# A depthwise convolution's second channel chunk moves to TensorE as products with diagonal matrices, beside attention in a two-layer backbone

## The chip, the cores and the metric

The kernel runs on one core of a Trainium2 chip. The metric is the device time of one execution in microseconds (us), lower is better. A core has TensorE (PE in the profile; PEld is its weight loads), VectorE (DVE), ScalarE (ACT), GpSimd (POOL) and SyncE (SP, which here issues most of the transfers). Each engine works through its own queue in order.

## The reference, cut to what matters

Two layers, shared by 512 latent and 128 context tokens, with 1024 channels:

```python
h = _rms(x, norm_g[0]) * (1 + sc1) + sh1
x = x + 0.5 * g1 * _swiglu(h, ffn1_wi, ffn1_wo)
h = _rms(x, norm_g[1]) * (1 + sc2) + sh2
u = h @ w_in                                   # 1536 columns
o_pool = _pool_mixer(u[..., :256], ...)
o_conv = _conv_mixer(u[..., 256:768], ...)
o_attn = attention(u[..., 768:])               # 8 heads, 5 blocks of 128 queries
x = x + g2 * (concat([o_pool, o_conv, o_attn]) @ w_out)
h = _rms(x, norm_g[2]) * (1 + sc3) + sh3
x = x + 0.5 * g3 * _swiglu(h, ffn2_wi, ffn2_wo)

def _conv_mixer(g, dw, db, norm_g, pw):
    glu = g[..., :256] * sigmoid(g[..., 256:])
    y = depthwise_conv(glu, dw, taps=31, centred) + db     # per channel
    return silu(_rms(y, norm_g)) @ pw
```

The nine vectors `sh1 ... g3` of a layer are SiLU(cond) @ mod_w + mod_b; each is 1024 columns of a 1024-row matrix.

## The kernel before, in words

Channels lie on the 128 partitions and tokens along the free dimension, so the 256 channels of the convolution are two chunks (c = 0 and 1). A dense product is done with a high and a low part of each operand in the type float32r, three products each (`product`, line 368). A layer is a feed-forward stage, the mixer (`mixer`, line 789), and a second feed-forward stage.

The mixer first makes the convolution's gate and value, keys, values and half of the queries from `u` (`ORDER`, line 54). Then it goes through 20 steps: four query chunks c, each with the five query blocks of `BATCHES` as two batches (line 1162 on). `batch` (line 1062) is attention's chain: scores on PE (L1085), mask and maximum on DVE (L1088), exponential on ACT (L1096), sum and reciprocal on DVE (L1097, L1098), scaling on ACT (L1100), transposes on PE (L1103) and their copies on ACT (L1104), products with the values on PE (L1110). It is written with a higher priority than what is laid beside it: the other half of the queries (q1), the pooling (pl), and the first part of the output product over w_out (`out_chunks`, part 0, tiles p_a and p_b), all paced by `PLAN`. The rest of w_out (tile p, L748) comes behind the 20 steps, with the second feed-forward stage.

Three more things ride on the steps, and the change touches all three:

- **Modulation.** Sixteen pieces of mod_w (vectors 5, 7, 6, 8; four pieces each), paced by `FILL` (line 44). A piece is a transfer of 1 MB issued on SP into one of two buffers (tag "raw", shared with the w_in and w_out loads) and eight float32 products (L269) into the one PSUM bank with the tag "x" (`BANKS`, line 46). After four pieces DVE reads the bank out.
- **Taps.** `conv_taps` (line 925) adds 31 shifted, scaled copies of the gated input `glu` into `cy`, one tile of 128x655 for each chunk; the 655 columns are 512 latent and 128 context tokens with 15 zero columns between. `TAP_PLAN` says how many taps of which chunk go with each step, and `behind` ties a tap to the batch's last reciprocal on DVE (chunk 0) or its last copy on ACT (chunk 1). Chunk 0 and the last four taps of chunk 1 are one DVE instruction each (L935; the first tap is L933). Taps 1 to 26 of chunk 1 are a scaled copy on ACT (L938, tile cm) and an add on POOL (L939):

```python
elif c == 0 or tp > POOL_TAPS:
    V.scalar_tensor_tensor(out=y, in0=src, scalar=wt, in1=y, ...)
else:
    A.activation(out=m, in_=src, func=AF.Copy, scale=wt)
    G.tensor_tensor(out=y, in0=y, in1=m, op=ALU.add)
```

- **The rest of the convolution.** `convolution` (line 1022) starts at step `CONV_AT` = 15 and does one piece per step: squares (L1024, L1025, tiles cacc and csq), the sum over channels on PE (L322, rc_ss), the spread of the scale (L334, rc_a and rc_b), swish, and the pointwise product (tiles cp_a, cp_b).

POOL also does rotary products for the queries (L824, L825) and the pooling sums (L980 to L988). A scheduler sets the order of each engine's queue from the written order and the priorities.

Of the kernel before, what the change touches and what calls it, by code (L numbers as in the profile page):

```python
# [9 lines left out]
F32 = mybir.dt.float32  # L10
F32R = mybir.dt.float32r
I32 = mybir.dt.int32
AF = mybir.ActivationFunctionType
ALU = mybir.AluOpType
PSUM = bass.MemoryType.PSUM

P = 128
# [10 lines left out]
TAPS = 31  # L28
# [8 lines left out]
COUT = NLAT + CPAD + NCTX  # L37
PPAD = 8
PLEN = PPAD + NLAT + PPAD + NCTX + PPAD
TMP = 688  # L40

FILL = (1, 0, 1, 1, 1, 1, 2, 1, 1, 2, 1, 1, 2, 1, 0, 1, 1, 2, 2, 1)
FILL_MODS = ((5, 7, 6, 8), (), (5, 7, 6, 8))
BANKS = {"a": 3, "s": 2, "t": 1, "o": 1, "x": 1}
AHEAD = 200
NOW = 400
BEHIND_BY = 0
BUFS = {"act": 6, "tmp": 7, "half": 9, "w": 3, "raw": 2}  # L50
POOL_TAPS = 26
CONV_AT = 15
TAP_PLAN = ((3, 2, 1, 2, 3, 2, 0, 2, 2, 1, 3, 2, 0, 2, 1, 3, 1, 1, 1, 3), (2, 4, 3, 3, 4, 4, 4, 2, 0, 4, 1, 1, 0, 1, 2, 1, 2, 0, 1, 4))
ORDER, BEHIND = ("cg", "kv", "q0", "ca"), ("q1", "pl")
PLAN = (0, 1, 0, 1, 0, 2, 0, 1, 0, 0, 0, 1, 1, 1, 2, 1, 1, 1, 1, 0)

# [42 lines left out]
def backbone(ctx: ExitStack, tc: tile.TileContext, ins, consts, y_prompt, y_sample, out_k, out_v):  # L99
    nc = tc.nc  # L100
    V, A, G, PE = nc.vector, nc.scalar, nc.gpsimd, nc.tensor
# [4 lines left out]
    scope = {}  # L106
# [12 lines left out]
    def bank(name, tag="o"):  # L119
        return psum.tile([P, 512], F32, tag=tag, name=name, bufs=BANKS[tag])  # L120
# [12 lines left out]
    def act(shape, dt, name):  # L133
        return work.tile(shape, dt, tag="act", name=name, padded_shape=[P, 2, T] if len(shape) == 3 else [P, 2 * T], bufs=BUFS["act"])
# [7 lines left out]
    ident = con[:, C_ID - C_EDGE:C_ID - C_EDGE + P]  # L142
# [4 lines left out]
    def transposed(rows, name, srcs, queue):  # L147

        t = tmp(name + "_r", P)
        for r0, src in srcs:  # L150
            n = src.shape[0]
            queue.dma_start(out=t[r0:r0 + n, 0:src.shape[1]], in_=src)
        ps = bank(name + "_ps")
        PE.transpose(ps[:, :rows], t[:rows, :], ident[:rows, :rows])
        o = one.tile([P, rows], F32, name=name)
        V.tensor_copy(o, ps[:, :rows])
        return o
# [15 lines left out]
    def bias_of(l, queue):  # L173
# [3 lines left out]
    vec = transposed(60, "vec", [  # L177
        (0, ins["norm_g"].rearrange("l j (k p) -> (l j k) p", p=P)),
        (48, ins["pool_scale"].rearrange("l (k p) -> (l k) p", p=P)),
        (52, ins["conv_b"].rearrange("l (k p) -> (l k) p", p=P)),  # L180
        (56, ins["conv_norm_g"].rearrange("l (k p) -> (l k) p", p=P)),
    ], nc.scalar)
# [17 lines left out]
    for i in range(5):  # L200
        xt = act([P, D], F32, f"xt{i}")
        src = ins["x_sample"][0, i * P:(i + 1) * P, :] if i < 4 else ins["x_prompt"][0]
# [83 lines left out]
    def mod_steps(l, vs, summed=True):  # L286
        return [f for v in vs for f in modulation(l, v, summed)]
# [478 lines left out]
    def into_ffn(l, j, wi, nm, load, mv, gate):  # L766

        acc = tmp(f"acc{l}{j}")
        inp = Input(l, j)
        scale_of(l, j, inp.a)  # L770
        f = Ffn(l, j, inp, wi)

        def then(h, sq):
            if h:
                plain_products(f, 0)
            with tc.high_priority(offset=NOW):
                pb = rstd_half(acc, sq, h, f"r{l}{j}{h}")
                for kp in range(4):
                    (inp.second if h else inp.first)(pb, kp)
            if h:  # L780
                for kp in range(4):
                    inp.sums(kp)
                plain_products(f, 1)

        last_group(nm, load, mv, gate, acc, then)
        return f


    def mixer(l, xa, R, tab, fill):
        w_in = ins["w_in"][l]  # L790
        taps, qkg, sink, nsink = (par[n] for n in ("taps", "qkg", "sink", "nsink"))
# [114 lines left out]
        glu = []  # L906
# [12 lines left out]

        QS, rq = {}, {}  # L920

        ys = [scope["pool"].tile([P, COUT], F32, tag="sg", name=f"cy{l}{c}", padded_shape=[P, TMP], bufs=3) for c in range(2)]
        todo = [list(range(TAPS)), list(range(TAPS))]

        def conv_taps(c, n, behind=None):

            for tp in todo[c][:n]:
                y = ys[c]
                wt = taps[:, (l * TAPS + tp) * 2 + c:(l * TAPS + tp) * 2 + c + 1]
                src = glu[c][:, tp:tp + COUT]  # L930
                with tc.issue_after(behind.ins) if behind is not None else ExitStack():
                    if tp == 0:
                        V.tensor_scalar(out=y, in0=src, scalar1=wt, scalar2=vec[:, 52 + 2 * l + c:53 + 2 * l + c], op0=ALU.mult, op1=ALU.add)  # L933
                    elif c == 0 or tp > POOL_TAPS:
                        V.scalar_tensor_tensor(out=y, in0=src, scalar=wt, in1=y, op0=ALU.mult, op1=ALU.add)  # L935
                    else:
                        m = scope["pool"].tile([P, COUT], F32, tag="sg", name=f"cm{l}{tp}", padded_shape=[P, TMP], bufs=3)
                        A.activation(out=m, in_=src, func=AF.Copy, scale=wt)  # L938
                        G.tensor_tensor(out=y, in0=y, in1=m, op=ALU.add)  # L939
            del todo[c][:n]  # L940

        def query_heads(t, b, c):
            sq, qt = tmp(f"qsq{l}{c}"), tmp(f"qt{l}{c}")
# [217 lines left out]
        i = 0  # L1161
        for c in range(4):
            m = act([P, 2, T], F32R, f"mixa{l}{c}")
            mix[4 + c] = (m[:, 0, :], m[:, 1, :])
            for blks in BATCHES:
                with tc.high_priority(offset=AHEAD):
                    behind = batch(c, blks, m)
                for _ in blks:
                    for _ in range(FILL[i]):
                        if fill:  # L1170
                            with tc.high_priority(offset=-BEHIND_BY):
                                fill.pop(0)()
                    for cc in range(2):
                        conv_taps(cc, TAP_PLAN[cc][i], behind[cc])
                    if i == CONV_AT:
                        for cc in range(2):
                            conv_taps(cc, TAPS, behind[cc])
                        conv = convolution()
                    if i >= CONV_AT:
                        next(conv, None)  # L1180
                    for _ in range(PLAN[i]):
                        next(bg)
                    i += 1
# [28 lines left out]
    f = Ffn(0, 0, inp, ins["ffn1_wi"][0])  # L1212
# [38 lines left out]
    for l in range(DEPTH):  # L1251
# [26 lines left out]
        ffn(f, ins["ffn1_wo"][l], gate1, after1, fill)  # L1278
        R = rstd(st["acc"], float(D), f"r{l}1")
        f = mixer(l, st["xa"], R, st["tab"], mod_steps(l, (5, 7, 6, 8), False))  # L1280

        g3 = gate_of(l, 2, 0.5)
# [15 lines left out]
        if not last:  # L1298
# [6 lines left out]
            f = into_ffn(l + 1, 0, ins["ffn1_wi"][l + 1], f"o{l}2_3", load, lambda k: (hid[lo + k][:, 0, :], hid[lo + k][:, 1, :]), g3)  # L1305
# [27 lines left out]
```

## Time and profile before

| | us |
|---|---|
| median of 3 runs | 2453.72 (2448.52 to 2455.20) |
| the profiled execution | 2454.21 |
| its span in the trace | 2452.4 |
| PE busy, share of the span | 2340.1, 95% |
| DVE busy | 1706.3, 70% |
| ACT busy | 1023.1, 42% |
| POOL busy | 462.5, 19% |

The span runs from the first to the last instruction; the execution's own time is 1.8 us longer. A busy PE is not PE at its densest: matmuls are pipelined, and a matmul counts as busy from its start to its modelled end. The mixer's steps lie around 570 to 755 us in layer 0 and 1775 to 1968 us in layer 1.

### The profile page before, as it was taken

To read this page: it belongs to the slowest core of one execution; us is meant where nothing else is said; L and a number is where in the kernel's file an instruction comes from. 1 tells how busy PE (TensorE), PEld (TensorE's weight loads), DVE (VectorE), ACT (ScalarE), POOL (GpSimd) and SP (SyncE) were. 2 spreads that over 40 slices of the span, in tenths; PEclk is the share of its full clock that TensorE was granted. 3 is DMA by queue.
4 is the path that set the end of the run, shared out by engine and by line. 5 is a ranking of instruction groups with operands and counts; after the bars stand their busy time and mean duration, and the time that the engine had idled before them with its cause. 6 is when DMAs were issued, how large, how long until landed. Compare 5 with 4: busy or idle time off the path is not lost.

```text
span 2452.4 us, 40409 instructions
## 1 busy us (share of the span) xinstructions
PE 2340.1 (95%) x16479; PEld 2218.7 (90%) x16479; DVE 1706.3 (70%) x3160; ACT 1023.1 (42%) x1867; POOL 462.5 (19%) x369
## 2 busy tenths in 40 slices
PE   7999999999789899999989999999997889999999
PEld 6999999997568899999989999999974789999998
DVE  7649495858866857585778585857588669585855
ACT  5324242426664533333354242424357545242423
POOL 2102020202531202020131111112024222020210
PEclk8999999999989999999999999999998899999999
DMA  7442422323402133333312424223243022222222
GB/s 236 140 154 83 142 83 75 100 91 123 163 22 78 52 115 123 112 117 118 115 41 85 142 82 142 78 86 102 73 149 129 31 70 81 75 82 91 78 78 78
DMA packets 193989, 246.03 MB, mean 100 GB/s; under 512 B 5705, under 2 KB 176494, under 8 KB 193804
## 3 DMA queue, kind: packets, MB, share of 16 engines
q1 hardware_dynamic: 191824, 240.81, 30.0%
q8 instruction: 129, 2.11, 0.4%
q0 software_dynamic: 512, 1.95, 0.3%
q10 hardware_dynamic: 1468, 0.70, 0.1%
q14 instruction: 56, 0.46, 0.1%
HBM read 240.55 MB, written 2.88 MB: 99 GB/s over the span
## 4 chain that ended last, share of the span: by engine, by line
PE 82%; DVE 11%; ACT 4%; issue 2%; DMA 1%; POOL 0%; SPq 0%; ACTq 0%; DVEq 0%
PE f_B L560 11%; PE o_a L378 11%; PE f_C L560 11%; PE f_A L560 11%; PE o_b L378 11%; PE f_D L560 6%; PE f L601 3%; PE p L748 2%; PE mod L269 2%; DVE cy L935 1%; PE u_q_b L378 1%; PE u_q_a L378 1%; DVE xa_l L396 1%; PE o L748 1%; ACT a_2S L1096 1%
## 5 line engine op out<-in xcount | busy, mean ns | idle before, releaser
L378 PE MATMUL o_a<-f_h,o_wh 128*128 128x320 f32 x1344 | 403.7, 311 | 0.0
L378 PE MATMUL o_b<-f_h,o_wh 128*128 128x320 f32 x1344 | 401.8, 310 | 0.0
L420 DVE SCALAR_TENSOR_TENSOR X<-o_a,gate,X 128x320 f32<-128x320 f32 x120 | 65.8, 549 | 303.6 <-PE o_a L378 303.3
L378 PEld LDWEIGHTS o_a<-f_h,o_wh 128*128 128x128 f32 x1344 | 251.2, 188 | 8.7 <-ACT o_wh L357 5.8
L357 ACT ACTIVATE o_wh<-wo 128x768 fp32r<-128x768 f32 (+1 forms) x120 | 95.9, 801 | 380.8 <-PE o_b L378 258.2
L378 PEld LDWEIGHTS o_b<-f_h,o_wh 128*128 128x128 f32 x1344 | 251.2, 188 | 2.9 <-issue 2.9
L552 POOL TENSOR_TENSOR f_t<-f 128x512 f32<-128x512 f32 x80 | 126.1, 1576 | 664.7 <-DMA f<-in_ffn_wi_dram 472.0
L659 POOL TENSOR_TENSOR f_t<-f_t,f 128x512 f32<-128x512 f32 x80 | 111.1, 1389 | 638.8 <-DVE f_q_wl L538 333.4
L378 PE MATMUL o_b<-f_h,o_wl 128*128 128x320 f32 x672 | 207.6, 309 | 0.0
L378 PE MATMUL o_a<-f_h,o_wl 128*128 128x320 f32 x672 | 207.5, 309 | 0.0
L536 ACT ACTIVATE f_q_wh<-f_t 128x512 fp32r<-128x512 f32 x140 | 85.8, 630 | 199.3 <-DVE f_t L550 54.6
L378 PEld LDWEIGHTS o_b<-f_h,o_wl 128*128 128x128 f32 x672 | 126.1, 188 | 0.0
L378 PEld LDWEIGHTS o_a<-f_h,o_wl 128*128 128x128 f32 x672 | 126.1, 188 | 0.0
L358 DVE TENSOR_TENSOR o_wl<-wo,o_wh 128x768 fp32r<-128x768 f32 (+1 forms) x120 | 108.1, 902 | 17.1 <-ACT o_wh L357 16.7
L536 ACT ACTIVATE f_P_wh<-f 128x512 fp32r<-128x512 f32 x112 | 66.4, 626 | 119.0 <-PE f_A L560 78.7
L939 POOL TENSOR_TENSOR cy<-cy,cm 128x655 f32<-128x655 f32 x52 | 86.9, 1672 | 145.4 <-ACT cm L938 145.4
L560 PE MATMUL f_B<-Fhf_h,f_q_wl 128*128 128x320 f32 x352 | 108.4, 308 | 0.8 <-DVE f_q_wl L538 0.8
L560 PE MATMUL f_B<-Fhf_h,f_q_wh 128*128 128x320 f32 x352 | 108.4, 308 | 0.2 <-ACT f_q_wh L536 0.2
L560 PE MATMUL f_B<-Fhf_l,f_q_wh 128*128 128x320 f32 x352 | 108.2, 308 | 0.0
L560 PE MATMUL f_C<-Fhf_h,f_m_wh 128*128 128x320 f32 x336 | 103.3, 308 | 0.0
L560 PE MATMUL f_C<-Fhf_l,f_m_wh 128*128 128x320 f32 x336 | 103.3, 308 | 0.0
L560 PE MATMUL f_C<-Fhf_h,f_m_wl 128*128 128x320 f32 x336 | 103.2, 308 | 0.0
(547 smaller groups left out, 7336.0 us busy)
## 6 DMA issues: line engine op xcount, KB each, us to landing
f<-in_ffn_wi_dram SPq DMA_DIRECT2D x88, 1024.0 KB, 5.2
mw<-in_mod_w_dram SPq DMA_DIRECT2D x72, 1024.0 KB, 5.5
wo<-in_ffn_wo_dram SPq DMA_DIRECT2D x48, 768.0 KB, 4.8
wo<-in_ffn_wo_dram SPq DMA_DIRECT2D x16, 512.0 KB, 3.4
wout<-in_w_out_dram SPq DMA_DIRECT2D x32, 256.0 KB, 3.3
win_q<-in_w_in_dram SPq DMA_DIRECT2D x4, 1024.0 KB, 5.2
xt<-in_x_sample_dram SPq DMA_DIRECT2D x4, 512.0 KB, 5.4
win_cg<-in_w_in_dram SPq DMA_DIRECT2D x2, 1024.0 KB, 5.3
```

Of the source, the lines that this page charges most:

```text
L269: PE.matmul(ps[32 * g:32 * g + 32, 0:256], C[:, k, :], w[:, :, g, :], start=(k == 0), stop=(k == KD - 1))
L357: A.activation(out=wh, in_=src, func=AF.Copy)
L358: V.tensor_tensor(out=wl, in0=src, in1=wh.bitcast(F32), op=ALU.subtract)
L378: PE.matmul(ps[:, :n], ww[:, k, :], xx[:, lo:lo + n], start=(k == order[0] and i == 0), stop=(k == order[-1] and i == 2))
L420: V.scalar_tensor_tensor(out=X[:, m, s:e], in0=ps[:, s - o:e - o], scalar=gate[:, m, c:c + 1], in1=X[:, m, s:e], op0=ALU.mult, op1=ALU.add)
L536: A.activation(out=h, in_=src, func=AF.Copy, scale=sign)
L552: G.tensor_tensor(out=t3, in0=self.block(g, 1, 1), in1=self.block(g, 0, 1), op=ALU.add)
L560: PE.matmul(ps[:, :HALF], w[:, kp, :], self.F[f][kp][:, i, :], start=(first and kp == 0 and n == 0), stop=(kp == 3 and n == 2), skip_group ...
L601: PE.matmul(ps[:, :HALF], w[:, k, :], x, start=(k == 0 and n == 0), stop=(k == KD - 1 and n == 2))
L659: G.tensor_tensor(out=t2, in0=t2, in1=self.block(g, 1, 0), op=ALU.add)
L748: PE.matmul(ps[:, :HALF], w[:, m % 2, k, :], x[:, h * HALF:(h + 1) * HALF], start=(k == 0 and n == 0), stop=(k == 3 and n == 2))
L939: G.tensor_tensor(out=y, in0=y, in1=m, op=ALU.add)
```

## The change

Chunk 0 keeps its 31 taps, all on DVE, in steps 0 to 10. Chunk 1 goes to PE: for each tap, POOL multiplies the identity with the tap's 128 weights (line 950 of the changed kernel, tile cd, four buffers), and PE multiplies this diagonal, as the stationary operand in float32, with the shifted columns of `glu` (line 951), summing over the 31 taps in a PSUM bank. One bank holds 512 columns, so the 655 columns go in two halves of 328 and 327, one after the other, in the bank with the tag "x"; ACT reads each half out with the bias. That makes 62 diagonals and 62 products in a layer, seven per step in steps 2 to 9 and six in step 10. The scaled copies on ACT and the adds on POOL are gone. `convolution` starts at step 11. Because the products hold the bank "x", `FILL` puts the four pieces of vector 5 into steps 0 and 1 and the other twelve into steps 10 to 19.

```diff
@@ -41,16 +41,16 @@
-FILL = (1, 0, 1, 1, 1, 1, 2, 1, 1, 2, 1, 1, 2, 1, 0, 1, 1, 2, 2, 1)
+FILL = (2, 2, 0, 0, 0, 0, 0, 0, 0, 0, 1, 2, 1, 1, 2, 1, 1, 1, 1, 1)
 FILL_MODS = ((5, 7, 6, 8), (), (5, 7, 6, 8))
 BANKS = {"a": 3, "s": 2, "t": 1, "o": 1, "x": 1}
 AHEAD = 200
 NOW = 400
 BEHIND_BY = 0
 BUFS = {"act": 6, "tmp": 7, "half": 9, "w": 3, "raw": 2}
-POOL_TAPS = 26
-CONV_AT = 15
-TAP_PLAN = ((3, 2, 1, 2, 3, 2, 0, 2, 2, 1, 3, 2, 0, 2, 1, 3, 1, 1, 1, 3), (2, 4, 3, 3, 4, 4, 4, 2, 0, 4, 1, 1, 0, 1, 2, 1, 2, 0, 1, 4))
+CONV_AT = 11
+
+TAP_PLAN = ((3, 2, 3, 3, 3, 3, 3, 3, 3, 3, 2), (0, 0, 7, 7, 7, 7, 7, 7, 7, 7, 6))
 ORDER, BEHIND = ("cg", "kv", "q0", "ca"), ("q1", "pl")
 PLAN = (0, 1, 0, 1, 0, 2, 0, 1, 0, 0, 0, 1, 1, 1, 2, 1, 1, 1, 1, 0)
@@ -919,25 +919,39 @@
         QS, rq = {}, {}
-        ys = [scope["pool"].tile([P, COUT], F32, tag="sg", name=f"cy{l}{c}", padded_shape=[P, TMP], bufs=3) for c in range(2)]
-        todo = [list(range(TAPS)), list(range(TAPS))]
-
-        def conv_taps(c, n, behind=None):
-
-            for tp in todo[c][:n]:
-                y = ys[c]
+        ys = [scope["pool"].tile([P, COUT], F32, tag="sg", name=f"cy{l}{c}", padded_shape=[P, TMP], bufs=2) for c in range(2)]
+        todo = [list(range(TAPS)), []]
+
+        def conv_taps(n, behind):
+
+            c, y = 0, ys[0]
+            for tp in todo[0][:n]:
                 wt = taps[:, (l * TAPS + tp) * 2 + c:(l * TAPS + tp) * 2 + c + 1]
                 src = glu[c][:, tp:tp + COUT]
-                with tc.issue_after(behind.ins) if behind is not None else ExitStack():
+                with tc.issue_after(behind.ins):
                     if tp == 0:
                         V.tensor_scalar(out=y, in0=src, scalar1=wt, scalar2=vec[:, 52 + 2 * l + c:53 + 2 * l + c], op0=ALU.mult, op1=ALU.add)
-                    elif c == 0 or tp > POOL_TAPS:
+                    else:
                         V.scalar_tensor_tensor(out=y, in0=src, scalar=wt, in1=y, op0=ALU.mult, op1=ALU.add)
-                    else:
-                        m = scope["pool"].tile([P, COUT], F32, tag="sg", name=f"cm{l}{tp}", padded_shape=[P, TMP], bufs=3)
-                        A.activation(out=m, in_=src, func=AF.Copy, scale=wt)
-                        G.tensor_tensor(out=y, in0=y, in1=m, op=ALU.add)
-            del todo[c][:n]
+            del todo[0][:n]
+
+        halves = ((0, 328), (328, COUT))
+        todo[1] = [(h, tp) for h in range(2) for tp in range(TAPS)]
+        conv_ps = {}
+
+        def conv_products(n):
+
+            c, y = 1, ys[1]
+            for h, tp in todo[1][:n]:
+                o, e = halves[h]
+                if tp == 0:
+                    conv_ps[h] = bank(f"cv{l}{h}", "x")
+                dg = scope["pool"].tile([P, P], F32, tag="dg", name=f"cd{l}{h}_{tp}", bufs=4)
+                G.tensor_scalar(out=dg, in0=ident, scalar1=taps[:, (l * TAPS + tp) * 2 + c:(l * TAPS + tp) * 2 + c + 1], scalar2=None, op0=ALU.mult)
+                PE.matmul(conv_ps[h][:, :e - o], dg, glu[c][:, tp + o:tp + e], start=(tp == 0), stop=(tp == TAPS - 1))
+                if tp == TAPS - 1:
+                    A.activation(out=y[:, o:e], in_=conv_ps[h][:, :e - o], func=AF.Identity, bias=vec[:, 52 + 2 * l + c:53 + 2 * l + c])
+            del todo[1][:n]
         def query_heads(t, b, c):
             sq, qt = tmp(f"qsq{l}{c}"), tmp(f"qt{l}{c}")
@@ -1170,11 +1184,12 @@
                         if fill:
                             with tc.high_priority(offset=-BEHIND_BY):
                                 fill.pop(0)()
-                    for cc in range(2):
-                        conv_taps(cc, TAP_PLAN[cc][i], behind[cc])
+                    if i < CONV_AT:
+                        conv_taps(TAP_PLAN[0][i], behind[0])
+                        with tc.high_priority(offset=-BEHIND_BY):
+                            conv_products(TAP_PLAN[1][i])
                     if i == CONV_AT:
-                        for cc in range(2):
-                            conv_taps(cc, TAPS, behind[cc])
+                        assert not todo[0] and not todo[1]
                         conv = convolution()
                     if i >= CONV_AT:
                         next(conv, None)
```

PE's queue just behind the value product of the convolution, layer 0. Before, the pieces of vector 5 (L269) stand singly between the products of the second half of the queries (u_q):

```order
L378 MATMUL u_q_a<-xa_h,u_q_wl 128x320
L378 MATMUL u_q_b<-xa_h,u_q_wl 128x322
L269 MATMUL mod_5_5949<-mw_5_2_6159,C 32x256 x8
L1085 MATMUL a_0_2s_6044<-KS_5186,QS_5663 128x512 x2
L378 MATMUL u_q_a<-xa_h,u_q_wh 128x320
```

And now (cv is the bank of the convolution's products, cd a diagonal):

```order
L1099 MATMUL a_0_2s_6066<-KS_5186,QS_5663 128x512 x2
L269 MATMUL mod_5_5949<-mw_5_3_5981,C 32x256 x8
L951 MATMUL cv_6159<-glu_5863,cd_0_6160 128x328
L951 MATMUL cv_6159<-glu_5863,cd_1_6163 128x328
L951 MATMUL cv_6159<-glu_5863,cd_2_6166 128x328
L951 MATMUL cv_6159<-glu_5863,cd_3_6169 128x328
L1099 MATMUL a_0_2s_6071<-KS_5186,QS_5663 128x384 x2
L1099 MATMUL a_0_2s_6076<-KS_5186,QS_5663 128x384 x2
L951 MATMUL cv_6159<-glu_5863,cd_4_6172 128x328
L951 MATMUL cv_6159<-glu_5863,cd_5_6175 128x328
L951 MATMUL cv_6159<-glu_5863,cd_6_6178 128x328
L378 MATMUL u_q_a<-xa_h,u_q_wh 128x320
```

All four pieces of vector 5 stand ahead of the first product with a diagonal, and seven of these ahead of u_q.

PE's queue in the middle of attention, layer 0. Before, in the second query chunk, pieces of the last vector (8) fill between scores, transposes and value products:

```order
L1103 MATMUL a_1_2t_6692<-con,a_1_2S_6652 128x128 x4
L1085 MATMUL a_2_2s_6965<-KS_5187,QS_6277 128x512 x2
L269 MATMUL mod_8_6932<-mw_8_0_6930,C 32x256 x8
L269 MATMUL mod_8_6932<-mw_8_1_7055,C 32x256 x8
L1085 MATMUL a_2_2s_6970<-KS_5187,QS_6277 128x384 x2
L1103 MATMUL a_1_2t_6699<-con,a_1_2S_6657 128x128 x4
```

Now the second half's products end only in the third chunk (a_2), and the first pieces of vector 7 come behind them:

```order
L951 MATMUL cv_6646<-glu_5863,cd_28_6960 128x327
L1124 MATMUL a_2_0o<-a_2_0S_6868,VS_5184 64x128
L951 MATMUL cv_6646<-glu_5863,cd_29_6963 128x327
L951 MATMUL cv_6646<-glu_5863,cd_30_6966 128x327
L1117 MATMUL a_2_0t_6908<-con,a_2_0S_6878 128x128 x4
L1124 MATMUL a_2_0o<-a_2_0S_6873,VS_5184 64x128
L1124 MATMUL a_2_0o<-a_2_0S_6868,VS_5184 64x128
L1124 MATMUL a_2_0o<-a_2_0S_6873,VS_5184 64x128
L1124 MATMUL a_2_0o<-a_2_0S_6868,VS_5184 64x128
L1124 MATMUL a_2_0o<-a_2_0S_6873,VS_5184 64x128
L269 MATMUL mod_7_6940<-mw_7_0_6938,C 32x256 x8
L269 MATMUL mod_7_6940<-mw_7_1_6970,C 32x256 x8
```

So twelve pieces (vectors 7, 6 and 8) have moved from ahead of this place to behind it.

POOL's queue around the rotary products of a query chunk (L824, L825), layer 0, before:

```order
L939 TENSOR_TENSOR cy_5189<-cy_5189,cm_5973 128x655
L824 TENSOR_TENSOR qr_sh<-qr_sh,tab_4857 128x512
L825 TENSOR_TENSOR u_q_t<-u_q_t,tab_4857 128x512
L939 TENSOR_TENSOR cy_5189<-cy_5189,cm_5976 128x655
L939 TENSOR_TENSOR cy_5189<-cy_5189,cm_6150 128x655
```

And now:

```order
L950 TENSOR_SCALAR cd_20_6328<-con,taps 128x128
L950 TENSOR_SCALAR cd_21_6412<-con,taps 128x128
L824 TENSOR_TENSOR qr_sh<-qr_sh,tab_4857 128x512
L825 TENSOR_TENSOR u_q_t<-u_q_t,tab_4857 128x512
L950 TENSOR_SCALAR cd_22_6415<-con,taps 128x128
L950 TENSOR_SCALAR cd_23_6418<-con,taps 128x128
```

Diagonals, which PE waits for, stand where the adds stood.

## Rows read from the trace of the kernel before

**Rows 1.** The page's head, then part 1: busy time, share of the span, instructions.
```profile
span 2452.4 us, 40409 instructions
PE 2340.1 (95%) x16479; PEld 2218.7 (90%) x16479; DVE 1706.3 (70%) x3160; ACT 1023.1 (42%) x1867; POOL 462.5 (19%) x369
```

**Rows 2.** Windows of both mixers: length, PE, PEld, DVE, ACT, POOL busy, PEclk, DMA, GB/s.
```profile
571.00:640.00 69.00, 62.58 (x487) 48.10 (x489) 56.07 (x144) 43.05 (x94) 19.94 (x18) 0.95 0.42 145
640.00:671.50 31.50, 19.37 (x165) 11.69 (x157) 29.60 (x49) 22.11 (x44) 17.50 (x14) 0.95 0.49 170
671.50:754.60 83.10, 72.86 (x448) 60.09 (x448) 52.91 (x124) 52.13 (x112) 21.94 (x14) 0.86 0.10 31
1774.60:1860.00 85.40, 76.15 (x568) 58.30 (x570) 73.32 (x179) 50.77 (x107) 26.45 (x27) 0.94 0.46 160
1860.00:1900.00 40.00, 29.07 (x208) 17.74 (x204) 31.07 (x63) 29.94 (x66) 19.14 (x12) 0.83 0.28 95
1900.00:1967.80 67.80, 58.83 (x382) 51.05 (x381) 42.22 (x97) 39.65 (x83) 17.68 (x12) 0.87 0.12 38
```

**Rows 3.** Windows: one stretch of dense products in a feed-forward stage.
```profile
480.00:490.00 10.00, 10.00 (x70) 10.00 (x69) 10.00 (x18) 7.34 (x12) 5.42 (x3) 1.00 0.32 107
```

**Rows 4.** Chain of waits around 1940 us, layer 1 (start, length, what).
```profile
1934.38 0.74 ACT cm L938
1935.19 1.58 POOL cy L939
...
1943.07 0.75 ACT csq L1025
1943.82 0.39 ACT a_2S L1104
...
1945.57 1.95 PE rc_ss L322 x10
```

**Rows 5.** Timeline of PE: float32 products of 128x320 among others.
```profile
780.62 0.70 PE L452 MATMUL r_b<-r_dg,ones 128*128 128x320 f32 x2
780.91 0.55 PE L748 MATMUL p<-mixa,p_h 128*128 128x320 f32 x1
781.30 0.31 PE L748 MATMUL p<-mixa,p_l 128*128 128x320 f32 x1
781.45 0.31 PE L748 MATMUL p<-mch,p_h 128*128 128x320 f32 x1
...
1750.83 0.75 PE L857 MATMUL rkb_a<-rkd,ones 128*64 128x320 f32 x2
1751.42 0.70 PE L857 MATMUL rkb_b<-rkd,ones 128*64 128x320 f32 x2
```

**Rows 6.** Timeline of PE: one modulation step.
```profile
601.52 1.07 PE L269 MATMUL mod<-mw,C 128*32 128x256 f32 x16
```

**Rows 7.** Tile: the tap instructions (ns, min/median/max).
```profile
L935 DVE SCALAR_TENSOR_TENSOR cy<-glu,taps,cy x68: 854/898/2318, 580.2 to 1942.1; 128x655 f32<-128x655 f32 x68
L939 POOL TENSOR_TENSOR cy<-cy,cm x52: 1571/1602/2107, 598.5 to 1937.7; 128x655 f32<-128x655 f32 x52
...
L938 ACT ACTIVATE cm<-glu,taps x52: 824/835/861, 597.6 to 1936.8; 128x655 f32<-128x655 f32 x52
```

**Rows 8.** Groups by form and by line: POOL's tensor_scalar.
```profile
L462 POOL TENSOR_SCALAR hf_q<-hf_q,a,modv 128x128 f32<-128x128 f32 x16 | 13.4, 837 | 0.0
...
L462 POOL TENSOR_SCALAR hf_q<-hf_q,a,modv x32: 442/506/2201, 29.0 to 2022.6; 128x192 f32<-128x192 f32 x16, 128x128 f32<-128x128 f32 x16
```

**Rows 9.** Tile p_wl: one DVE shape beside a busy and an idle POOL.
```profile
L358 DVE TENSOR_TENSOR p_wl<-wout,p_wh x16: 674/694/2084, 664.3 to 1929.7; 128x512 fp32r<-128x512 f32 x16
L741 DVE TENSOR_TENSOR p_wl<-wout,p_wh x12: 681/684/693, 749.7 to 1968.9; 128x512 fp32r<-128x512 f32 x12
```

**Rows 10.** Parts 2 and 6 of the page: GB/s in 40 slices; one DMA issue.
```profile
GB/s 236 140 154 83 142 83 75 100 91 123 163 22 78 52 115 123 112 117 118 115 41 85 142 82 142 78 86 102 73 149 129 31 70 81 75 82 91 78 78 78
...
wout<-in_w_out_dram SPq DMA_DIRECT2D x32, 256.0 KB, 3.3
```

## The prediction

> **What bounds the kernel now.** I read the page's head first. PE is busy 95% of the span, so outside the mixer there is nothing that this change could shorten, and inside it every microsecond of new PE work needs a gap [rows 1]. Then I cut each layer's mixer steps into three stretches [rows 2]: the first with q1, the pooling products and the beginning of attention; the second, in which PE has little but attention; the third with the last two query chunks and the first part of w_out. The cut between second and third is where the third chunk's first transposes run.
>
> The reader is to see three things there. In the first stretch PE is nearly full: 62.58 of 69.00 us in layer 0, 76.15 of 85.40 in layer 1. In the second it is not (19.37 of 31.50, 29.07 of 40.00), while DVE is (29.60 of 31.50, 31.07 of 40.00): attention's chain and the taps queue on DVE, and PE waits. In the third PE is busy again, at a granted clock of 0.86 and 0.87. Idle PE in the three stretches is 6.4, 12.1 and 10.2 us in layer 0 and 9.3, 10.9 and 9.0 us in layer 1, 57.9 us together. In layer 1 the convolution itself ends late: the chain runs through a scaled copy on ACT, an add on POOL, taps on DVE and the square csq, from 1934.38 to 1943.82, and attention's own copy of its transposes (a_2S, L1104) sits on ACT behind that square [rows 4].
>
> **The change part by part.** *Products.* 62 in a layer, 124 in all. The trace has no such product of 328 columns, but two kin. A float32 product of 320 columns starts 0.59 us before the next one of its kind [rows 5]. Another one, r_b, stands in a stream of float32r products that start 0.15 us apart; from its start to 781.30 there are 0.68 us with one such product in between, which leaves 0.53. The whole recorded length of a pair of passes is 0.75 at most. I take the first, scaled to 328 columns: 0.60; the ends are 0.53 and 0.75. A half is 31 x 0.60 = 18.6 us, a layer 37.2, against 28.8 (layer 0) and 29.2 (layer 1) of idle PE.
>
> *Pieces of modulation.* One piece is 1.07 us of PE [rows 6]. Twelve pieces, 12.8 us, leave the first two stretches and enter the third: by the order, four from the first (4.3 us) and eight from the second (8.6). The four of vector 5 stay in the first, only earlier.
>
> *The sum on PE.* I let each stretch absorb new work up to its idle time, and lengthen by the rest. First stretch: +18.6 - 4.3 = 14.3; beyond the idle time that is 7.9 us in layer 0 and 5.0 in layer 1. Second: +18.6 - 8.6 = 10.0, which is less than 12.1 and 10.9: nothing. Third: +12.8, which is 2.6 and 3.9 beyond. Together 7.9 + 5.0 + 2.6 + 3.9 = 19.4 us. With 0.53 for a product only the first stretch shrinks, by 2.2 us twice: 15.0. With 0.75 the first stretch gives 12.6 + 9.7, the second 2.6 + 3.8, the third 6.5 as before: 35.2.
>
> *Taps on DVE.* Chunk 0's 31 stay and chunk 1's last four go: four times 0.898 us less in a layer [rows 7]. But the plan before has 21 taps of chunk 0 and four of chunk 1 by step 10, the new one all 31, so six more, 5.4 us, fall before the third stretch. DVE's idle time in the first stretch is 12.9 us, enough; in the second only 1.9. I take nothing, with 5.4 a layer as the upper end. What leaves the third stretch is off the path if PE is full there.
>
> *ACT and POOL.* ACT loses 26 copies of 0.835 us, 21.7 a layer, and gains two evictions, each half as wide as such a copy. POOL loses 26 adds of 1.60, 41.7 us, and gains 62 diagonals. Neither engine is full in any stretch (ACT 29.94 of 40.00 at most, POOL 17.50 of 31.50), so I credit nothing; where their work stood on the path, rival 1 takes it up.
>
> *The added wait.* PE now waits for POOL, and the diagonals have four buffers, so POOL is at most four products ahead. Queued behind a late diagonal on PE are attention's transposes and scores; queued on POOL behind a diagonal that waits for a free buffer are the rotary products of later query chunks, which the third and fourth chunk of attention need. POOL's nearest instruction, a tensor_scalar with a pointer scalar, has a median of 0.506 us and for 128x128 a mean of 0.837 [rows 8]. The median covers a product of 0.60; the mean does not. I take the median, since a diagonal has one scalar and the row's form two, and keep the mean for rival 2.
>
> One DVE shape tells why mean and median differ: p_wl takes 0.684 us where POOL rests and up to 2.084 where POOL adds [rows 9]. [...]
>
> *Transfers and the bank.* Twelve pieces of 1 MB now load in the third stretch, which moved 31 and 38 GB/s; 12.6 MB more make 183 and 224 GB/s, still under the 236 of the span's first slice [rows 10]. SP's queue has the last w_out loads behind the last pieces of vector 8; one takes 3.3 us to land. I take zero and keep 3.3 a layer. The first piece of vector 7 waits until ACT has read the second half out of the bank; attention's transposes and value products lie between, so nothing.
>
> The sum, 19.4 us, goes on the profiled execution, 2454.2: 2473.6. The median of the runs lies 0.5 lower, so the forecast is 2473 us, 0.8% slower. With all upper ends (35.2 + 10.8 + 6.6 = 52.6) it is 2507; with the lower price of a product, 2469.
>
> **The rivals.** *1, faster: the late convolution leaves the chain and PE packs the products in.* For it: the 9.4 us of layer 1 in which ACT, POOL and DVE finish chunk 1 go away altogether [rows 4], since the plan has its products done by step 10. And a busy PE is loosely packed: weight loads fill 246.97 us of the six stretches, the matmul row 318.85 [rows 2], where in a dense stretch both read 10.00 of 10.00 [rows 3]. The difference, 71.9 us, could hold what the idle time cannot (74.4 - 57.9 = 16.5). Then the PE term is zero. [...] Against the rival: in the first stretch, where half of the products go, the clock is 0.95 and 0.94 and idle time is scarce. It decides where the products fit between attention's instructions without making them late.
>
> *2, much slower: diagonals come too slowly.* At 0.837 us, 62 diagonals are 51.9 us of POOL in a layer, 14.7 more than the products take; PE would wait that long, in a queue in which attention stands behind it: 2473.6 + 2 x 14.7 = 2503. [...] Against: POOL has 49 of 69 us free in the first. It decides at 0.60 us, the price of a product.
>
> *3, no change: DVE remains the bound.* The second stretch is DVE's already, and if the first is so in effect, products run under DVE's work and neither engine's sum counts: 2454, and 2461 with 3.6 us a layer for waits that move from one engine to the other. Against: PE's 62.58 of 69.00 in the first stretch.
>
> **How the numbers follow.** The forecast's case (2462 to 2492) has 0.42, rival 1 (2434 to 2446) 0.25, rival 2 (2492 to 2510) 0.17, rival 3 (2446 to 2461) 0.16. A measurement of this kernel can tell about 0.3%, 7.4 us, from no change. So faster is rival 1 with a sliver of rival 3, 0.26; same the rest of rival 3 and the forecast's lower edge, 0.17; slower 0.57. The range 2440 to 2502 leaves out half of rival 1 and less than half of rival 2, some 0.2.
>
> **What would show it.** Products (L951) that start 0.60 us apart where they stand together; the first stretch longer by 5 to 8 us with PE busy nearly throughout; the second no longer; PE's idle time in it halved. If PE's idle time before L951 is released by POOL, rival 2 is right; a tensor_scalar on POOL that takes over 0.60 on average says the same. Rival 1 would show as a granted clock near 1.0 in all stretches and rc_ss well before attention's last chunk, with stretches no longer than now. The forecast is wrong if the products take under 0.5 us, or if the mixer ends earlier than it does now.

## The result, and the profile after

The changed kernel takes 2477.82 us (median of four runs, 2476.00 to 2480.67) against 2453.16 (2448.52 to 2455.20) for the kernel before on the same chip: a ratio of 1.0104, 95% interval 1.0088 to 1.0120, or 24.7 us longer. The forecast was 2473. The number held; the way to it, as the runs below show, did not.

The head and part 1 of the page after, which answer to [rows 1]:

```profile
span 2474.2 us, 40923 instructions
PE 2392.1 (97%) x16727; PEld 2250.1 (91%) x16727; DVE 1667.6 (67%) x3150; ACT 989.1 (40%) x1819; POOL 481.8 (19%) x441
```

PE gained 52.0 us of busy time, DVE lost 38.7 and ACT 34.0; POOL, with diagonals for adds, has 19.3 more. To see where in the mixer the time went, I cut both kernels at events that both have: the first product of u_cg, the end of the second query chunk (its last write of mixa), and the first product of tile p. Windows of before, layer 0 and then layer 1 (length, PE, PEld, DVE, ACT, POOL busy, PEclk, DMA, GB/s):

```profile
489.50:674.00 184.50, 163.39 (x1177) 135.67 (x1176) 140.13 (x326) 93.69 (x186) 50.76 (x47) 0.95 0.36 125
674.00:749.50 75.50, 65.42 (x401) 53.78 (x402) 46.79 (x107) 48.51 (x104) 20.36 (x13) 0.84 0.08 25
1701.50:1887.90 186.40, 167.49 (x1178) 136.69 (x1176) 141.63 (x327) 92.57 (x186) 50.73 (x46) 0.93 0.36 124
1887.90:1961.80 73.90, 62.66 (x403) 52.64 (x403) 44.85 (x108) 48.63 (x105) 21.11 (x14) 0.86 0.08 26
```

The same four of the changed kernel:

```profile
491.60:669.60 178.00, 170.92 (x1088) 143.80 (x1087) 133.32 (x324) 82.46 (x170) 74.41 (x89) 1.00 0.18 62
669.60:763.40 93.80, 83.53 (x617) 60.32 (x616) 36.28 (x109) 42.66 (x97) 2.76 (x4) 0.95 0.43 144
1716.60:1903.00 186.40, 179.48 (x1114) 150.26 (x1116) 133.56 (x324) 82.93 (x172) 74.84 (x90) 0.97 0.18 59
1903.00:1985.20 82.20, 76.87 (x609) 56.84 (x601) 34.85 (x108) 41.89 (x97) 1.70 (x2) 0.98 0.48 164
```

Read the first column first. The part with nearly all the products got no longer: 184.5 to 178.0 us in layer 0, 186.4 in both in layer 1. The part behind it did: by 18.3 and 8.3 us. The four lengths add up to 520.3 before and 540.4 after, 20.1 of the 21.8 us between the spans. (Of the rest, 2.1 us lie ahead of the first mixer, 489.5 to 491.6; the same product starts anywhere from 488.4 to 491.3 us in the runs below, so I put them down to scatter.) Then the PE column: its idle time, length less busy, falls from 61.3 to 29.6 us, and its busy time rises by 51.8.

What fills the end can be read from PE's groups in the last chunk of layer 0 (699.5 to 770.1 us after):

```profile
L269 PE MATMUL mod<-mw,C 128*32 128x256 f32 x112 | 11.9, 423 | 1.5 <-DMA mw<-in_mod_w_dram 1.4
L378 PE MATMUL p_a<-mixp,p_wh 128*128 128x320 f32 x28 | 9.0, 376 | 5.4 <-ACT p_wh L357 5.4
```

and before (713.0 to 750.9 us), where there is no piece of modulation at all:

```profile
L378 PE MATMUL p_a<-mixp,p_wh 128*128 128x320 f32 x12 | 2.9, 329 | 0.0
```

Pieces of modulation and the first part of w_out have gathered there. The chain of waits of the changed kernel has loads in that part, in layer 0

```profile
677.65 6.58 DMA mw<-in_mod_w_dram
...
697.94 5.07 DMA mw<-in_mod_w_dram
...
717.89 3.39 DMA wout<-in_w_out_dram
...
763.89 4.22 DMA wout<-in_w_out_dram
```

and in layer 1:

```profile
1903.65 4.96 DMA mw<-in_mod_w_dram
...
1919.94 6.74 DMA mw<-in_mod_w_dram
...
1954.29 2.99 DMA wout<-in_w_out_dram
...
1967.23 3.21 DMA wout<-in_w_out_dram
```

Last, the new instructions. On the chain (start, length, what), products take 0.55 us each; a product is two records:

```profile
589.92 0.55 PE cv L951 x2
...
600.59 1.66 PE cv L951 x6
```

The tile of the diagonals (ns, min/median/max), with what ended its engines' idle time (us, times):

```profile
L950 POOL TENSOR_SCALAR cd<-con,taps x124: 596/661/2244, 464.5 to 1897.6; 128x128 f32<-128x128 f32 x124
its engine sat idle before it (us, times) until:
  PE cv L951: 60.3, 24
...
  POOL cd L950: 7.3, 13
...
who waited for it (us, times):
...
  PEld cv L951: 4.9, 9
  PE cv L951: 2.4, 4
```

and the groups by line of the diagonals and of VectorE's taps (count, busy us, mean ns, idle before):

```profile
L950 POOL TENSOR_SCALAR cd<-con,taps 128x128 f32<-128x128 f32 x124 | 105.0, 859 | 69.0 <-PE cv L951 60.3 <-DVE u_pl_t L415 8.0
...
L935 DVE SCALAR_TENSOR_TENSOR cy<-glu,taps,cy 128x655 f32<-128x655 f32 x60 | 58.2, 970 | 1.1
```

In all, POOL waits 60.3 us for PE to free a buffer. PE waits far less for a diagonal: the 7.3 us are 4.9 us before weight loads and 2.4 before products, and each of the products' four waits lies inside a wait of a weight load, so PE waits 4.9 us at most.

One stretch is different. In the second half of layer 1's products the chain of waits runs on POOL,

```profile
1867.35 0.60 POOL cd L950
...
1869.43 9.16 POOL cd L950 x9
...
1893.07 2.34 POOL cd L950 x2
...
1895.45 0.82 PE cv L951 x2
```

and the window there reads

```profile
1867.00:1896.00 29.00, 27.00 (x143) 18.48 (x142) 25.02 (x51) 18.29 (x43) 28.28 (x32) 1.00 0.00 1
```

Diagonals take 20.2 us of this chain and the pooling sums between them 7.0. POOL is full, and PE fills its time with other work.

### The profile page after: what moved, and what is told of

It reads as the page before. It is cut to its first block, busy times and chain, and to the rows that moved or that the text cites. A ratio compares the mean times of both kernels' runs of the same rounds, so it can differ in the third digit from the quotient of the medians.

```text
span 2474.2 us, 40923 instructions
## 1 busy us (share of the span) xinstructions
PE 2392.1 (97%) x16727; PEld 2250.1 (91%) x16727; DVE 1667.6 (67%) x3150; ACT 989.1 (40%) x1819; POOL 481.8 (19%) x441
## 4 chain that ended last, share of the span: by engine, by line
PE 85%; DVE 7%; DMA 2%; ACT 2%; POOL 1%; issue 1%; ACTq 0%; SPq 0%; DVEq 0%; POOLq 0%
PE f_B L560 11%; PE f_C L560 11%; PE o_a L378 11%; PE f_A L560 11%; PE o_b L378 11%; PE f_D L560 6%; PE f L601 3%; PE mod L269 3%; PE p L748 2%; PE cv L951 2%; PE u_q_b L378 1%; PE u_q_a L378 1%; PE p_a L378 1%; DVE xa_l L396 1%; PE p_b L378 1%
## 5 line engine op out<-in xcount | busy, mean ns | idle before, releaser
L950 POOL TENSOR_SCALAR cd<-con,taps 128x128 f32<-128x128 f32 x124 | 105.0, 859 | 69.0 <-PE cv L951 60.3
```

The costliest lines, as they stand in the source:

```text
L950: G.tensor_scalar(out=dg, in0=ident, scalar1=taps[:, (l * TAPS + tp) * 2 + c:(l * TAPS + tp) * 2 + c + 1], scalar2=None, op0=ALU.mult)
```

## The experiments

All ratios are to the kernel before, run anew with each group of experiments (medians 2452.87 for e1 to e4, 2453.51 for e5 to e8, 2453.16 for e9 to e12). The first theories were W (the bill is PE's work) and T (the bill is the late loads).

**The pieces alone, and the products alone.**

```diff
(e1, kernel before)
+FILL = ...   (that of the changed kernel)
(e2, changed kernel)
                 o, e = halves[h]
+                if 0 < tp < TAPS - 1:
+                    continue
```

> The kernel before, with nothing but the pacing of the modulation pieces (FILL) taken from the changed kernel: twelve of the sixteen pieces of a layer come in steps 10 to 19. The taps stay on DVE, ACT and POOL. Theory W (work on PE: the change is paid for by the 34 us of products a layer, and moved pieces cost only what PE cannot absorb in the third stretch): slower than before by the 2.6 + 3.9 = 6.5 us of the prediction's third stretch, about 2460 us. Theory T (transfers: in the changed kernel's layer 0, 5.07, 3.39 and 4.22 us of loads of mod_w and w_out stand on the chain in the last two chunks, because the pieces and the w_out loads now share two buffers late): slower than before by 15 us or more, 2468 to 2475.

> The changed kernel with only the first and the last of the 31 taps of each half as products; 58 of 62 diagonals and products of a layer are left out, so the second chunk's convolution is not computed in full. Everything else, pacing included, is as in the changed kernel. Removed on PE: 58 x 0.555 = 32 us a layer, 64 us together. Theory W: the 20 us that the change cost come back, and perhaps more, since PE has been full: 2440 to 2456 us. Theory T: the products lie where attention was ahead anyway and the last chunk still waits for its loads: 2466 us or more.

e1: 2464.38 us, ratio 1.0043 (1.0028 to 1.0058): 7 to 14 us slower, 11.2 by the medians, between the two theories. e2: 2429.13, 0.9904 (0.9889 to 0.9919): 48.7 us below the changed kernel, more than its whole loss, so T falls as the main cause. A product together with its diagonal, since e2 leaves out both, costs 48.7 / 116 = 0.42 us of the run. What I had not expected is e2 against e1: with late pieces in both, the taps' move off VectorE, ACT and POOL had brought 35.3 us.

**The loads.**

```diff
(e3, changed kernel)
-            raw = wpool.tile([P, 2, D], F32, tag="raw", ...)
-            nc.sync.dma_start(out=raw, ...)
+            if t == 0 or v not in (7, 6, 8):
+                st["raw"] = wpool.tile([P, 2, D], F32, tag="raw", ...)
+                nc.sync.dma_start(out=st["raw"], ...)
+            raw = st["raw"]
(e4, changed kernel)
+FILL = (2, 2, 0, 0, 0, 0, 2, 2, 0, 0, 0, 0, 1, 1, 1, 1, 1, 1, 1, 1)
+CONV_AT = 12
+TAP_PLAN = ((3, 2, 3, 3, 3, 3, 3, 3, 3, 3, 2, 0), (0, 0, 8, 8, 8, 7, 0, 0, 8, 8, 8, 7))
```

> The changed kernel in which the four pieces of each of the three late vectors (7, 6, 8) use the data of the first one: 9 of 12 late loads of 1 MB a layer are left out, so these vectors are not the right ones, but PE does all 12 pieces. Theory W: within 4 us of the changed kernel's 2477.8. Theory T: the 5.07 + 3.39 + 4.22 = 12.7 us of loads on layer 0's chain go, and about as much in layer 1: 2452 to 2462 us.

> The changed kernel with the four pieces of vector 7 between the two halves of the products (first half in steps 2 to 5, pieces in steps 6 and 7, second half in steps 8 to 11, the rest of the convolution from step 12, eight pieces in steps 12 to 19): a third of the late pieces is taken back to the middle. Theory W: PE's work is the same, within 4 us of 2477.8. Theory T: a third of the late loads less, 4 to 9 us faster, 2469 to 2474.

e3: 2471.92, 1.0077 (1.0062 to 1.0092), 5.9 us below the changed kernel: W's 4 us were passed, T's 15 or more not reached. The loads that I showed on the changed kernel's chain add up to 37.2 us; in the same part of e3's chain there is one,

```profile
698.24 3.25 DMA wout<-in_w_out_dram
```

so the chain lost some 34 us of loads and the run 5.9. Other work took their place on the chain; a load's length on it is not what the load costs. e4: 2475.74, 1.0092 (1.0077 to 1.0107): its interval overlaps the changed kernel's, so taking a third of the late pieces back gives nothing that can be told.

**What the second chunk's taps cost before, and what the diagonals cost after.**

```diff
(e5, kernel before)
             for tp in todo[c][:n]:
+                if c == 1 and 0 < tp <= POOL_TAPS:
+                    continue
(e6, changed kernel)
+                if tp == 0:
+                    conv_ps["dg"] = scope["pool"].tile([P, P], F32, tag="dg", ...)
+                dg = conv_ps["dg"]
-                G.tensor_scalar(out=dg, ...)
+                if tp == 0: G.tensor_scalar(out=dg, ...)
```

> The kernel before with taps 1 to 26 of the second chunk left out (the 26 copies on ACT and 26 adds on POOL of a layer); their share of the convolution is not computed. No products, pieces paced as before. Theory F (freed engines: the copies and adds held up attention and PE with it; between the runs e1_late_pieces and e2_few_products 35.3 us went although 8 products came in): 2415 to 2425 us. Theory N (the prediction's credit of nothing for ACT and POOL; the gain of e2_few_products came from the order of its queues and from the chunk's end on DVE): 2445 to 2454 us.

> The changed kernel with one diagonal for each half instead of 31: 60 of 62 POOL instructions of a layer are left out and all products of a half use the first tap's weights, so the convolution's numbers are wrong in the second chunk. PE's products, the pacing and the transfers stay. Theory W (PE's work): PE waited 7.3 us for diagonals in all, so 0 to 6 us faster than the changed kernel, 2472 to 2478. [...]

e5: 2418.73, 0.9872 (0.9848 to 0.9897): theory F. The 52 copies and 52 adds of the two layers had cost 34.8 us. e6: 2463.66, 1.0046 (1.0029 to 1.0063): the 120 diagonals cost 14.2 us of the changed kernel, outside theory W's range. That is three times what PE is seen to wait for them (4.9 us, not the 7.3 that I had written down).

**Two mixtures.** Both compute everything, with fewer products in steps 2 to 5 and the pieces from step 6.

```diff
(e7 and e8, changed kernel; PROD = 11 and 15)
+        def rest_taps(n, behind):
+            for tp in todo[2][:n]:
...
+(e7)                V.scalar_tensor_tensor(out=y, in0=src, scalar=wt, in1=y, ...)
+(e8)                A.activation(out=m, in_=src, func=AF.Copy, scale=wt)
+(e8)                G.tensor_tensor(out=y, in0=y, in1=m, op=ALU.add)
```

> The full computation. Of the second chunk's 31 taps the first 11 are products on PE (22 a layer, steps 2 to 5, in the bank x, read out with the bias), the other 20 are VectorE instructions on the read-out tile in steps 6 to 14; nothing on ACT or POOL but the diagonals. The pieces of vectors 7, 6, 8 begin at step 6 again; the rest of the convolution starts at step 15. Theory W with freed engines: 40 of 62 products of a layer less than the changed kernel, at 48.7 us / 116 = 0.42 us each 33.6 us, and most of the 10 us of late pieces back, against 40 more VectorE taps of 0.86 us where that engine has gaps: 2435 to 2450 us. If VectorE is the bound as soon as it gets 16 taps a layer more than in the kernel before: 2455 us or more.

> The full computation. As e7_hybrid_dve, but 15 taps of the second chunk as products (30 a layer) and the other 16 as before on ACT and POOL (scaled copy and add; the copy is in a tile with the tag tmp), in steps 6 to 14. Theory W with freed engines: 32 of 62 products a layer less than the changed kernel, 27 us, most of the 10 us of late pieces back, and 16 of the 26 copies and adds come back, for which at most 16/26 of 35 us, 21 us, are lost: 2440 to 2460 us.

e7: 2441.55, 0.9953 (0.9937 to 0.9969): faster than before. e8: 2464.47, 1.0054 (1.0034 to 1.0073): with 16 taps back on ACT and POOL in place of 20 on VectorE, the gain is gone and more, over the range I gave. It has 16 products more than e7, some 7 us at 0.42, of the 22.9 us between the two. This pointed at POOL's adds.

**Adds or copies, and no products at all.**

```diff
(e9, kernel before)
-                        G.tensor_tensor(out=y, in0=y, in1=m, op=ALU.add)
(e10, kernel before)
-                        A.activation(out=m, in_=src, func=AF.Copy, scale=wt)
-                        G.tensor_tensor(out=y, in0=y, in1=m, op=ALU.add)
+                        G.tensor_tensor(out=y, in0=y, in1=src, op=ALU.add)
(e11, kernel before; both chunks behind the last reciprocal)
-POOL_TAPS = 26
+POOL_TAPS = 0
+TAP_PLAN = ((3, 2, 3, 3, 3, 3, 3, 2, 2, 2, 1, 1, 1, 1, 1, 0, 0, 0, 0, 0),
+            (0, 0, 1, 1, 1, 2, 2, 2, 2, 3, 3, 4, 4, 3, 3, 0, 0, 0, 0, 0))
-                        conv_taps(cc, TAP_PLAN[cc][i], behind[cc])
+                        conv_taps(cc, TAP_PLAN[cc][i], behind[0])
(e12, e7 with PROD = 6 and the plans for it)
-                G.tensor_scalar(out=dg, in0=ident, ...)
+                A.activation(out=dg, in_=ident, func=AF.Copy, scale=...)
```

> The kernel before with the 26 adds on POOL of a layer left out; the 26 scaled copies on ACT stay but are not used, so taps 1 to 26 of the second chunk are missing from the result. Theory L (POOL's adds slow VectorE: a tap takes 1.05 us on the mean before and 0.97 in the changed kernel, p_wl 1.13 and 0.69): most of the 34.8 us of e5_no_act_pool, 2418 to 2430 us. Theory A (ACT's copies stand ahead of attention's own work on ACT): at most 10 us of it, 2443 to 2454 us.

> The kernel before with the 26 scaled copies on ACT of a layer left out; the 26 adds on POOL stay and add the unscaled input, so the second chunk's numbers are wrong. Theory L: within 10 us of before, 2444 to 2454 us. Theory A: most of the 34.8 us, 2418 to 2430 us.

> The full computation, no products: the kernel before with all 62 taps of a layer on VectorE (none on ACT and POOL), behind attention's last reciprocal, the first chunk's in steps 0 to 14 and the second's in steps 2 to 14; pieces and the rest of the convolution as before. From e7_hybrid_dve, 22.8 us above e5_no_act_pool: 44 products at 0.42 us are 18.5 of it, which leaves 4 us for some 30 more VectorE taps. If taps stay that cheap, 52 more of them than in e5_no_act_pool cost 7 to 15 us: 2425 to 2434 us. If VectorE becomes the bound, at up to 0.86 us for each of the 52, 44.7 us: up to 2463 us.

> The full computation. As e7_hybrid_dve, with only 6 taps of the second chunk as products (12 a layer, steps 2 and 3), 25 on VectorE from step 4, the pieces from step 4 on, and the diagonals made on ACT in place of POOL. Against e7_hybrid_dve 20 products fewer at 0.42 us, 8.4 us, up to 5 us for the 44 POOL diagonals of e7_hybrid_dve (14.2 us for 120 in e6_one_diagonal), and 10 more VectorE taps at up to 0.86 us: 2428 to 2440 us.

e9: 2426.91, 0.9896 (0.9880 to 0.9912): without the adds 26.2 of the 34.8 us go; theory L. e10: 2459.86, 1.0036 (1.0024 to 1.0049): with the adds alone the kernel is 6.7 us slower than before, outside both ranges. The groups of VectorE's taps and of p_wl read, before,

```profile
L935 DVE SCALAR_TENSOR_TENSOR cy<-glu,taps,cy 128x655 f32<-128x655 f32 x68 | 71.5, 1051 | 1.1 <-POOL cy L939 0.2
...
L358 DVE TENSOR_TENSOR p_wl<-wout,p_wh 128x512 fp32r<-128x512 f32 x16 | 18.0, 1127 | 8.8 <-ACT p_wh L357 8.6
```

and in e9, without adds,

```profile
L935 DVE SCALAR_TENSOR_TENSOR cy<-glu,taps,cy 128x655 f32<-128x655 f32 x68 | 61.1, 907 | 0.5
```

where the tile p_wl (ns, min/median/max) has

```profile
L358 DVE TENSOR_TENSOR p_wl<-wout,p_wh x16: 649/682/693, 662.3 to 1911.0; 128x512 fp32r<-128x512 f32 x16
```

In e10 the adds no longer wait for copies:

```profile
L937 POOL TENSOR_TENSOR cy<-cy,glu 128x655 f32<-128x655 f32 x52 | 83.4, 1604 | 16.3 <-DVE cy L933 13.1
...
L935 DVE SCALAR_TENSOR_TENSOR cy<-glu,taps,cy 128x655 f32<-128x655 f32 x68 | 77.8, 1152 | 0.5
```

The same 68 instructions take 0.907, 1.051 and 1.152 us on the mean, as POOL adds beside them not at all, behind copies, or freely; p_wl takes at most 0.693 in e9, where its mean before was 1.127. One mean alone is a weak witness, though: in e5, also without adds, the taps read

```profile
L937 DVE SCALAR_TENSOR_TENSOR cy<-glu,taps,cy 128x655 f32<-128x655 f32 x68 | 65.1, 961 | 0.6
```

A better one is VectorE's whole busy time, since the kernel before, e5, e9 and e10 give it the same 3160 instructions. It is 1706.3 us before [rows 1], and in e5, e9 and e10

```profile
PE 2324.8 (96%) x16479; PEld 2203.1 (91%) x16479; DVE 1669.8 (69%) x3160; ACT 983.8 (41%) x1815; POOL 380.1 (16%) x317
...
PE 2329.4 (96%) x16479; PEld 2208.9 (91%) x16479; DVE 1665.8 (69%) x3160; ACT 1020.8 (42%) x1867; POOL 374.6 (15%) x317
...
PE 2339.9 (95%) x16479; PEld 2217.9 (90%) x16479; DVE 1716.8 (70%) x3160; ACT 986.3 (40%) x1815; POOL 457.8 (19%) x369
```

So the adds lengthen VectorE's work by 40.5 us where copies space them (before against e9) and by 47.0 where none do (e10 against e5). In run time they cost 26.2 and 41.1 us. Two other ways in which adds could cost time do not fit. One is the second chunk's late end [rows 4]: in e10 the last add starts at 1864.0 us and not at 1937.7, and the run is no shorter. The other is the rotary products that queue behind adds on POOL: before, ACT waits 20.1 us in all for the query tile made from these products, and in e9 19.6. How VectorE's longer work turns into run time I did not separate. In the four stretches of the two mixers, cut at the same events, e9 has in all

```profile
sum 491.40, PE 445.36 PEld 367.64 DVE 328.33 ACT 279.10 POOL 54.19; mean PE 111.34 PEld 91.91 DVE 82.08 ACT 69.77 POOL 13.55
```

so PE's idle time there is 46.0 us where it was 61.3, and its busy time 445.36 where it was 458.96, with nearly as many instructions (3135 and 3159).

e11: 2433.57, 0.9923 (0.9909 to 0.9938), 19.6 us faster than before and 44.3 faster than the change: the lowest median of the full kernels, with no product and nothing of the taps on ACT or POOL. It also places the first chunk's taps in other steps, which I did not test by itself. Its page:

```profile
span 2435.1 us, 40394 instructions
PE 2335.3 (96%) x16479; PEld 2215.5 (91%) x16479; DVE 1704.5 (70%) x3212; ACT 987.1 (41%) x1815; POOL 378.1 (16%) x317
```

VectorE does 52 more taps than before [rows 1] in 1.8 us less busy time. Its first mixer windows show no full engine:

```profile
490.60:667.20 176.60, 163.52 (x1178) 135.10 (x1176) 142.31 (x345) 82.59 (x172) 28.86 (x32) 0.95 0.36 131
667.20:738.20 71.00, 63.45 (x403) 52.16 (x403) 43.67 (x114) 40.59 (x93) 1.71 (x2) 0.88 0.09 27
```

e12: 2437.23, 0.9934 (0.9920 to 0.9949); its interval overlaps e11's, so 12 products a layer neither help nor hurt beyond what can be told.

## Why the prediction was right, and where its steps were not

The change's 24.7 us come apart by the medians along e1, e2 and the changed kernel, in this order: +11.2 for the late pieces (2453.2 to 2464.4), -35.3 for the taps off ACT, POOL and VectorE (to 2429.1), +48.7 for 58 of 62 products a layer with their diagonals (to 2477.8). The prediction's sum, +19.4, got near this by luck: products and pieces, put at 19.4, cost 59.9, and a gain that was put at nothing gave 35.3 back.

- **"Neither engine is full in any stretch ..., so I credit nothing"**: this step failed. Leaving out ACT's and POOL's share gave 34.8 us (e5), and leaving out the adds alone 26.2 (e9). POOL, busy for 19% of the span [rows 1], cost time all the same: with its adds VectorE's work was 40.5 us longer (before against e9). The trace of before had it. I took VectorE's tap at its median, 0.898, which hides the lengthened ones; the mean, 1.051, has them, and p_wl's 2.084 against 0.684 [rows 7, 9] was read as a warning about the diagonals and not as a price already being paid.
- **Idle time of PE as room for products**: by the traces the balance came out, 51.8 us of new busy time against 31.7 us of idle time gone. But the room was not free: in e9, 15.3 us of the idle time went without a product, and PE's busy time fell besides, from 458.96 to 445.36 us; why it fell no run separates. Measured on their own, products with their diagonals cost 48.7 us, not the 7.9 + 5.0 of the sum. By the difference to e6, some 34 of these are the products'.
- **Price of a product**: 0.55 on the chain, against 0.60 taken and 0.53 to 0.75 given.
- **Stretches**: the first was to grow by 7.9 and 5.0 us and the third by 2.6 and 3.9. Up to the end of the second chunk nothing grew; behind it 18.3 and 8.3 us came. I read it so: attention stands ahead in PE's queue by priority, and with VectorE less slowed it ran ahead; what PE could not hold was pushed to the end of the mixer, with w_out. No run tests this by itself.
- **Moved pieces, 6.5 us, and transfers, nothing, with 6.6 as the upper end**: the pieces cost 11.2 us alone (7 to 14 by the interval of e1), and in the changed kernel loads are worth 5.9 (e3), near the upper end for the transfers.
- **The added wait, nothing**: this step failed too. I took the median of a tensor_scalar, 0.506, as covered by a product; the diagonals have a mean of 0.859 (the group's row: 105.0 us for 124) and cost 14.2 us in all (e6). Rival 2 had the price of one right, 0.837. Its 14.7 us a layer are not seen: PE waits 4.9 us at most, and over most of the two stretches POOL waits for PE. But in the second half of layer 1's products POOL is full and on the chain for 27.2 us, as rival 2 has it, with the pooling sums in the same queue. Where the 14.2 us lie stays open: VectorE's busy time falls by 8.0 us in e6 (1667.6 to 1659.6 for the same 3150 instructions), and of the 15.3 us between the two spans only 5.0 are in the mixers as cut above.
- **Rival 1**: half of its mechanism came true. The late convolution left the chain (rc_ss starts at 700.5 us where it was 729.7), and the granted clock rose from 0.95, 0.84, 0.93, 0.86 to 1.00, 0.95, 0.97, 0.98 in the four windows, with PE busy for a larger share of each (89, 87, 90 and 85% before, 96, 89, 96 and 94% after). The lower end of rival 1's range, 2434, counts on time that a higher clock saves, and no run shows such a saving: here the clock rose and the time rose by 24.7 us, and e11, the fastest full kernel, has 0.88 in a window.

VectorE's busy time for the same 3160 instructions was 1716.8, 1706.3 and 1665.8 us, with adds free (e10), spaced (before) or absent (e9). The 2.084 us of p_wl beside an add [rows 9] spoke for removing the adds as much as against adding diagonals, and I had used it on one side only.

## What to carry to other kernels

Before you give an engine's idle time away, ask what made it idle: of 61.3 us of idle PE here, 15.3 went when POOL's adds went, with no product in their place. Compare the mean of an instruction with its median or minimum: a gap says that something lengthens some of them (the taps before: 1.051 against 0.898 us; p_wl: 1.127 against 0.694). What a neighbour takes is then shown by leaving the neighbour out and reading the whole busy time of the slowed engine for the same instructions, and it counts as a gain when the neighbour's work leaves: here 40.5 us of VectorE's time and 26.2 us of the run. And try the plainest place first: all 62 taps on VectorE beat the split over three engines by 19.6 us and the products on PE by 44.3.

## What the runs showed of the hardware

- The 52 adds of 128x655 on POOL, 1.60 us each at the median, lengthened VectorE's busy time for the same 3160 instructions by 40.5 us and the kernel by 26.2 (e9); taking away only the copies that spaced them made it 6.7 us slower (e10).
- A diagonal of 128x128 on POOL has a median of 0.661 us and a mean of 0.859; a VectorE tap of 128x655, with five times the columns, has 0.893 and 0.953 in e11.
- Fifty-two more VectorE taps lengthened the kernel by 14.8 us and VectorE's busy time by 34.7 (e11 against e5): VectorE at 142 of 177 us had room that its 70% on the page does not place.
